# Block buffers, prepared operands and norm chains in a hybrid decoder layer

## The chip, the core and the metric

The kernel runs on one core of a Trainium2 chip. The core has a matrix engine (TensorE, PE in the profile, with its weight loads as PEld), a vector engine (VectorE, DVE), an activation engine (ScalarE, ACT), a general engine (GpSimd, POOL) and a queue engine that issues transfers (SyncE, SP). Each works through its own instructions in order and waits for others by semaphores. The metric is the device time of one execution, in microseconds (us). Three runs are given as a median with the lowest and the highest.

## The reference

One layer of a post-norm decoder over 1024 tokens of 1024 columns: a mixer of a state-space group and a gated linear attention, then a cross-attention into 256 memory tokens, then a squared-ReLU MLP of 4096 hidden columns. Each is added to the scaled residual, and the sum is normalised over its row. The end of it is what this case is about:

```
h = layer_norm(DN_ALPHA * h + memory_cross_attention(...), ln2_g, ln2_b)
ff = jnp.square(jax.nn.relu(h @ w_ff1[l])) @ w_ff2[l]
h = layer_norm(DN_ALPHA * h + ff, ln3_g, ln3_b)
```

All arithmetic is float32. A layer norm takes mean and variance of each row, multiplies the centred row by the reciprocal root of the variance (the deviation, below), then by a gain, and adds a bias.

## The kernel before

The 1024 tokens are eight tiles of 128 rows, res(0) to res(7), each 1024 columns wide. A float32 matmul is made of three: each operand is split into a high half and a low half (`split`, line 150: ScalarE copies the high half, VectorE or GpSimd subtracts it to get the low half), and `mm3` (line 160) multiplies high by high, high by low and low by high.

**The second norm** (ln2) follows the cross-attention's output product, `dense(pa, ...)` at line 1378. It runs two column halves; in each, a block of 24 matmuls for each of the eight tiles. In the second half VectorE adds each block to the residual (`post_norm`, line 1209) and calls `layer_norm` (line 224). That takes the statistics (the first half's were taken ahead), computes the deviation by eight small VectorE operations (`rsqrt1`, line 172), and normalises the tile. It shares the work: VectorE centres and scales columns, ScalarE multiplies columns 512 to 1023 by the deviation, GpSimd adds their bias. In the light form (tiles 0, 2, 4, 5, bits of GLN), ScalarE also centres them, and GpSimd multiplies by the gain.

**The up product** (line 1609) is one level of a seven-product Strassen scheme: the tokens and the hidden columns are cut in halves, and 16 groups g of hidden columns need seven products each (UP, line 1329), 12 matmuls a product. For the first eight groups (EDGE) two products, which need only the first four tiles, are made first for all (products 0 to 15), and the other five later in blocks. The last eight groups take all seven in a block. Between products 3, 6, 9 and 12 and the next ones, `x_tile` (line 1295) transposes and combines tiles 4 to 7. Each product has one weight operand, split ahead by `w1_prep` (line 1351) into a buffer of the queue `upq`. It is prepared four products ahead of its use in program order (LEADU) and its buffer is appended again after it. Three operands are prepared during the second norm (`up_first`), and seven buffers are in use: three pairs in the pool of weights, and one in the buffer named kv. Sums and differences of weights (s1, s2, s3, s4) are made by VectorE; s1 and s2 have one buffer each (w1s).

The evictions of a product follow in `up_product` (line 1410). Several products add into one bank of the accumulator after its earlier content has been read: v1 (of k = 4) and v2 (of k = 2) are such reads by VectorE, and in the first sixteen products ScalarE's copy of k = 0 is another. The squared hidden blocks go into block buffers (`hid_block`), are stored to memory, and are loaded again for the down product. Four block buffers are used to begin with, and seven from product 16 on.

**The down product** (line 1638) runs seven passes k, each of eight steps over pairs of groups. Evictions, statistics and norms are hung into these steps as a list (`pend`), one entry a step. Statistics and norms of tiles 0 to 3 (`norm_half`) go into passes 5 and 6, one tile an entry, and `behind()` puts them behind VectorE's latest instruction. Pass 6 produces tiles 4 and 5 together, then 6, then 7 in two halves of columns. `last_norm` (line 1557) normalises one tile: a chain for its deviation, then VectorE, ScalarE and GpSimd, then two stores. For tile 7 VectorE does all.

The order of each engine's instructions is not the program's order. A planner simulates the program with costs of its own, and places an instruction on its engine as soon as it takes it for ready, the one earlier in the program first. So an instruction that the planner took for ready early can stand, on the chip, ahead of one that is ready earlier.

Of the kernel before, what the change touches and what calls it, by code (L numbers as in the profile page):

```python
# [7 lines left out]
F32 = mybir.dt.float32  # L8
F32R = mybir.dt.float32r
# [8 lines left out]
P = 128  # L18
# [63 lines left out]
def hybrid_layer(  # L82
# [89 lines left out]
    def rsqrt1(y, v, eps, t):  # L172
# [4 lines left out]
        for _ in range(3):  # L177
            stt(V, w, y, vh, y, ALU.mult, ALU.mult)
            stt(V, y, w, 1.5, y, ALU.add, ALU.mult)

    ident = const.tile([P, P], F32, name="ident")
    G.memset(ident, 0.0)
    G.affine_select(out=ident, in_=ident, compare_op=ALU.not_equal, fill=1.0, base=0,
# [37 lines left out]
        rsqrt1(tq[:, 0:1], mv[:, 1:2], EPS, tq[:, 1:3])  # L221
        return mv, tq

    def layer_norm(xt, rows, light=False, st=None):
        mv, tq = norm_stats(xt, st)
        lo_, hi_ = slice(0, 512), slice(512, D)
        if light:
            stt(V, xt[:, lo_], xt[:, lo_], mv[:, 0:1], rows[:, 0, lo_], ALU.subtract, ALU.mult)
            stt(V, tq[:, 3:4], mv[:, 0:1], -1.0, tq[:, 0:1], ALU.mult, ALU.mult)
            act(xt[:, hi_], xt[:, hi_], AF.Identity, scale=tq[:, 0:1], bias=tq[:, 3:4])  # L230
            tt(G, xt[:, hi_], xt[:, hi_], rows[:, 0, hi_], ALU.mult)
        else:
            stt(V, xt, xt, mv[:, 0:1], rows[:, 0, :], ALU.subtract, ALU.mult)
            act(xt[:, hi_], xt[:, hi_], scale=tq[:, 0:1])
        stt(V, xt[:, lo_], xt[:, lo_], tq[:, 0:1], rows[:, 1, lo_], ALU.mult, ALU.add)
        tt(G, xt[:, hi_], xt[:, hi_], rows[:, 1, hi_], ALU.add)
# [757 lines left out]
    def res(t):  # L994
        return R[t // 4][:, t % 4, :]
# [213 lines left out]
    def post_norm(put, rows, scale=ALPHA, ahead=False):  # L1209

        half = stage.tile([P, NT, 2, 6], F32, tag="cn", bufs=1, name="half") if ahead else None

        def epi(n, t, po):
            r = res(t)[:, n * 512:(n + 1) * 512]
            if scale is None:
                tt(V, r, r, po, ALU.add)
            else:
                stt(V, r, r, scale, po, ALU.mult, ALU.add)
            if n == 0:
                if ahead:  # L1220
                    V.bn_stats(out=half[:, t, 0, :], in_=r)
                late.append(lambda: None)
            else:
                layer_norm(res(t), rows, GLN >> t & 1, half[:, t] if ahead else None)
                late.append(lambda: put(t))
        return epi

# [139 lines left out]
    def up_first():  # L1367

        z = wp.tile([P, 2, 2, 512], F32R, tag="w", name="w1q")
        upq.extend(z[:, i] for i in range(2))  # L1370
        upq.append(stage.tile([P, 2, 512], F32R, tag="kv", bufs=1, name="w1q"))
        w1_load(0)
        w1_load(1)
        for u in ups[:3]:
            w1_prep(*u)


# [3 lines left out]
    for _ in range(2):  # L1381
        z = wp.tile([P, 2, 2, 512], F32R, tag="w", name="w1q")
        upq += [z[:, i] for i in range(2)]
    wr_, hb_ = (wp.tile([P, 4, 512], F32, tag="w", name=n) for n in ("w1s", "hid"))
    pr1 = rowp.tile([P, 4, 512], F32, tag="row", name="pr")
    sums, v1, v2 = (wr_[:, 0], wr_[:, 1]), wr_[:, 2], wr_[:, 3]

    blocks = [hb_[:, i] for i in range(4)]
    nblk = [0]

    def hid_block():
# [162 lines left out]
            j = n * 512 // nw + i  # L1554
            V.bn_stats(out=sts[t][:, j, :], in_=res(t)[:, j * nw:(j + 1) * nw])

    def last_norm(t):
        mv = small.tile([P, 2], F32, tag="mv", name="mv")
        tq = small.tile([P, 4], F32, tag="tq2", name="tq2")
        V.bn_aggr(out=mv, in_=sts.pop(t))  # L1560
        rsqrt1(tq[:, 0:1], mv[:, 1:2], EPS, tq[:, 1:3])
        for n in range(2):
            c = slice(n * 512, (n + 1) * 512)
            r, g_, b_ = res(t)[:, c], rows3[:, 0, c], rows3[:, 1, c]
            if t == NT - 1:
                stt(V, r, r, mv[:, 0:1], g_, ALU.subtract, ALU.mult)
                stt(V, r, r, tq[:, 0:1], b_, ALU.mult, ALU.add)
            elif n == 0 or t > 3:
                stt(V, r, r, mv[:, 0:1], g_, ALU.subtract, ALU.mult)
                act(r, r, scale=tq[:, 0:1])  # L1570
                tt(G, r, r, b_, ALU.add)
            else:
                stt(V, tq[:, 3:4], mv[:, 0:1], -1.0, tq[:, 0:1], ALU.mult, ALU.mult)
                act(r, r, AF.Identity, scale=tq[:, 0:1], bias=tq[:, 3:4])
                tt(G, r, r, g_, ALU.mult)
                tt(G, r, r, b_, ALU.add)
            nc.sync.dma_start(out=out[t * P:(t + 1) * P, c], in_=r)

    def norm_half(m):
        with behind():  # L1580
            for n in range(2):
                stats(m, n)
            last_norm(m)

    nl, npr = [0], [0]

# [18 lines left out]
        edge_cells.extend(more_cells(2))  # L1605
        down_ahead(2, 2)

    nw_ = 3
    for i, (j, g, k) in enumerate(ups):
        while nw_ < len(ups) and nw_ <= i + LEADU:  # L1610
            w1_load(ups[nw_][0] + 1)
# [26 lines left out]
    for k in range(6):  # L1638
# [10 lines left out]
        for m, _, _, po in banks:  # L1649
            pend.append(lambda k=k, m=m, po=po: evict(k, m, po))  # L1650
        if k == 4:
            for m in range(2):
                pend.extend((lambda m=m: norm_half(m), lambda: None))

    def last_half(m):
        nw = 256 if m == 3 else 512
        stats(4 + m, 1, nw)

    for m in range(2):
        pend.extend((lambda m=m: norm_half(2 + m), lambda m=m: (last_half(2 * m), last_half(2 * m + 1))))  # L1660
    for ms in ((0, 1), (2,), (3,)):
        parts = [(m, c, w) for m in ms for c, w in (((0, 256), (256, 256)) if m == 3 else ((0, 512),))]
        for part in ([parts] if len(ms) == 2 else [[z] for z in parts]):
# [7 lines left out]
            for m, c, w, po in banks:  # L1671
                r = res(4 + m)[:, c:c + w]
                tt(V, r, r, po, ALU.add)
                V.bn_stats(out=sts[4 + m][:, c // w, :], in_=r)  # L1674
                if c + w == 512:
                    last_norm(4 + m)


# [31 lines left out]
```

## Time and profile before

| | |
|---|---|
| median of 3 runs | 1414.79 us (1411.76 to 1419.1) |
| the profiled execution | 1412.6 us, of which its span 1410.8 us |
| TensorE busy (matmuls) | 1341.5 us, 95% of the span |
| VectorE busy | 998.0 us, 71% |
| ScalarE busy | 570.1 us, 40% |
| GpSimd busy | 460.0 us, 33% |
| granted clock of TensorE, mean | 0.986 |

A row of the time line gives the start and the duration in us, the engine, the line of the kernel, the operation, what it writes and reads, its shape, and how often it stands there in a row. In brackets is how long the engine was idle before it, and what ended that. A helper's line (L142, L145, L148, L163) stands for all its callers, so one goes by the names of the tiles: `hl` are weights, `R` the residual, `tq` the deviation, `w1q` an operand of the up product, `w1s` the weight sums and v1 and v2, `hid` the block buffers, `pr` and `p_d` the kept first products, `xd`, `xt`, `xb` the combined tokens, `cell`, `pb` the operands of the down product. A row of the waits gives the waiting engine and what it waited for, then us in total, times, and the longest.

### The profile page before, as it was taken

To read this page: it belongs to the slowest core of one execution; us is meant where nothing else is said; L and a number is where in the kernel's file an instruction comes from. 1 tells how busy PE (TensorE), PEld (TensorE's weight loads), DVE (VectorE), ACT (ScalarE), POOL (GpSimd) and SP (SyncE) were. 2 spreads that over 40 slices of the span, in tenths; PEclk is the share of its full clock that TensorE was granted. 3 is DMA by queue.
4 is the path that set the end of the run, shared out by engine and by line. 5 is a ranking of instruction groups with operands and counts; after the bars stand their busy time and mean duration, and the time that the engine had idled before them with its cause. 6 is when DMAs were issued, how large, how long until landed. Compare 5 with 4: busy or idle time off the path is not lost. (4 is left out here: it accounts for less than half of the span.)

```text
span 1410.8 us, 18927 instructions
## 1 busy us (share of the span) xinstructions
PE 1341.5 (95%) x6824; PEld 1112.6 (79%) x6824; DVE 998.0 (71%) x1783; ACT 570.1 (40%) x946; POOL 460.0 (33%) x338
## 2 busy tenths in 40 slices
PE   7798999999899998999998999999999999999997
PEld 6575788788898887788887777778888888888886
DVE  8999588756855489844478667766555676568797
ACT  4433532342545143333123654445545343335431
POOL 1663144312855133200014223443332142003364
PEclk9899999999999999999999999999999999999999
DMA  9722342543756120310120656554446985334432
GB/s 311 255 110 81 107 121 52 161 159 112 255 186 209 56 73 23 119 30 1 60 60 23 194 174 198 194 188 142 145 140 230 343 270 178 104 105 150 149 105 90
DMA packets 155513, 199.81 MB, mean 142 GB/s; under 512 B 16294, under 2 KB 86044, under 8 KB 155292
## 3 DMA queue, kind: packets, MB, share of 16 engines
q1 hardware_dynamic: 143536, 179.44, 39.5%
q10 hardware_dynamic: 11884, 19.17, 3.7%
q8 instruction: 54, 0.88, 0.3%
q14 instruction: 39, 0.32, 0.1%
HBM read 140.38 MB, written 58.20 MB: 141 GB/s over the span
## 5 line engine op out<-in xcount | busy, mean ns | idle before, releaser
L163 PE MATMUL ps_d<-xt,w1q 128*128 128x512 f32 x576 | 138.3, 391 | 9.8 <-DVE w1s L142 9.5
L163 PEld LDWEIGHTS ps_d<-xt,w1q 128*128 128x128 f32 x576 | 107.3, 188 | 35.4 <-issue 12.2
L142 POOL TENSOR_TENSOR hl<-raw,hl 128x1024 fp32r<-128x1024 f32 x21 | 63.0, 3006 | 168.3 <-ACT hl L148 168.2
L163 PE MATMUL ps_s<-cell 128*128 128x512 f32 x432 | 113.0, 389 | 0.0
L163 PE MATMUL ps_d<-cell 128*128 128x512 f32 x432 | 106.0, 389 | 0.4 <-DVE hid L142 0.4
L142 POOL TENSOR_TENSOR R<-R,row 128x512 f32<-128x512 f32 x42 | 57.8, 1386 | 138.4 <-ACT R L148 134.9
L163 PE MATMUL ps_d<-h0T,hl 128*128 128x512 f32 x384 | 93.6, 402 | 5.8 <-DVE hl L142 5.8
L163 PE MATMUL ps_g<-xb,w1q 128*128 128x512 f32 x384 | 94.3, 397 | 3.9 <-ACT hid L148 3.9
L163 PE MATMUL ps_d<-hl,y 128*128 128x512 f32 x384 | 95.1, 403 | 2.5 <-DVE y L142 2.5
L163 PEld LDWEIGHTS ps_d<-cell 128*128 128x128 f32 x432 | 81.0, 188 | 17.6 <-DVE hid L142 0.8
L163 PEld LDWEIGHTS ps_s<-cell 128*128 128x128 f32 x432 | 81.1, 188 | 16.8
L163 PEld LDWEIGHTS ps_d<-h0T,hl 128*128 128x128 f32 x384 | 73.2, 193 | 25.8 <-DVE hl L142 6.2
L163 PE MATMUL ps_d<-hl,h0T 128*128 128x512 f32 x384 | 91.1, 393 | 1.4 <-DVE h0T L142 1.3
L148 ACT ACTIVATE hl<-raw 128x1024 fp32r<-128x1024 f32 x62 | 64.8, 1059 | 66.1 <-PE ps_d L163 60.2
L163 PE MATMUL ps_d<-hl,p 128*128 128x512 f32 x384 | 89.0, 391 | 0.0
L163 PEld LDWEIGHTS ps_g<-xb,w1q 128*128 128x128 f32 x384 | 72.5, 191 | 19.6 <-ACT hid L148 4.7
L163 PEld LDWEIGHTS ps_d<-hl,y 128*128 128x128 f32 x384 | 72.6, 193 | 18.0 <-DVE y L142 3.0
L148 ACT ACTIVATE hid<-hid 128x512 f32<-128x512 f32 x112 | 70.8, 632 | 36.9 <-DVE hid L142 35.1
L163 PEld LDWEIGHTS ps_d<-hl,h0T 128*128 128x128 f32 x384 | 71.0, 188 | 17.3 <-DVE h0T L142 1.8
L163 PEld LDWEIGHTS ps_d<-hl,p 128*128 128x128 f32 x384 | 71.6, 188 | 14.6
L142 DVE TENSOR_TENSOR cell<-ha,cell 128x1024 fp32r<-128x1024 f32 x56 | 78.2, 1401 | 5.6 <-ACT cell L148 3.4
L148 ACT ACTIVATE w1q<-raw 128x512 fp32r<-128x512 f32 x80 | 50.0, 628 | 76.2 <-PE ps_d L163 39.6
(286 smaller groups left out, 2868.8 us busy)
## 6 DMA issues: line engine op xcount, KB each, us to landing
g_d<-hid SPq DMA_DIRECT2D x112, 256.0 KB
ha<-g_d SPq DMA_DIRECT2D x56, 512.0 KB
raw<-in_w_ff_dram SPq DMA_DIRECT2D x40, 512.0 KB
b<-in_w_ff_dram SPq DMA_DIRECT2D x32, 512.0 KB
raw<-in_w_mkv_dram SPq DMA_DIRECT2D x16, 512.0 KB
raw<-in_w_in_dram SPq DMA_DIRECT2D x16, 512.0 KB
wq<-in_w_mq_dram SPq DMA_DIRECT2D x8, 512.0 KB
xs<-in_x_dram SPq DMA_DIRECT2D x8, 512.0 KB
```

The source lines that it names most:

```text
L142: e.tensor_tensor(out=o, in0=a, in1=b, op=op)
L148: A.activation(out=o, in_=i, func=f, **kw)
L163: PE.matmul(o, lhs(i), rhs(j), start=first and n == 0, stop=last and n == 2, skip_group_check=more)
```

## The change

- Up product: `up_first` prepares two operands instead of three, and kv no longer holds an operand, so that six operand buffers are in use. kv becomes two more block buffers: six to begin with, nine from product 16 on.
- Second norm: for tiles 5, 6 and 7, VectorE normalises the whole tile by two operations on 1024 columns. ScalarE and GpSimd have no part in it.
- Final norms: `last_stats` computes the deviations of several tiles in one chain (`rsqrt_n`, with nine steps of three kinds instead of six, each on as many columns as there are tiles). Tiles 0 to 3 share one, and tiles 4 and 5 share one; 6 and 7 keep a chain of their own. The statistics of tiles 0 and 1 and of 2 and 3 now stand in one entry each, and the norms of tiles 0 and 1 in the two entries after them. The second column half of tiles 0 to 3 is normalised as the first: VectorE centres and multiplies by the gain, ScalarE multiplies by the deviation, GpSimd adds the bias, where ScalarE had centred and GpSimd had multiplied by the gain.

```diff
+    def rsqrt_n(y, v, eps, t):
+        n = y.shape[1]
+        vh, w = t[:, 0:n], t[:, n:2 * n]
+        ts(V, vh, v, eps, -0.5, ALU.add, ALU.mult)
+        ts(V, y.bitcast(I32), vh.bitcast(I32), -0.5, 1597463007.0 - 2.0 ** 30 - 2.0 ** 22, ALU.mult, ALU.add)
+        for _ in range(3):
+            tt(V, w, y, y, ALU.mult)
+            tt(V, w, w, vh, ALU.mult)
+            stt(V, y, w, 1.5, y, ALU.add, ALU.mult)
...
-    def layer_norm(xt, rows, light=False, st=None):
+    def layer_norm(xt, rows, light=False, st=None, alone=False):
         mv, tq = norm_stats(xt, st)
         lo_, hi_ = slice(0, 512), slice(512, D)
+        if alone:
+            stt(V, xt, xt, mv[:, 0:1], rows[:, 0, :], ALU.subtract, ALU.mult)
+            stt(V, xt, xt, tq[:, 0:1], rows[:, 1, :], ALU.mult, ALU.add)
+            return
...
-                layer_norm(res(t), rows, GLN >> t & 1, half[:, t] if ahead else None)
+                layer_norm(res(t), rows, GLN >> t & 1, half[:, t] if ahead else None, ahead and t > 4)
...
-        upq.append(stage.tile([P, 2, 512], F32R, tag="kv", bufs=1, name="w1q"))
         w1_load(0)
         w1_load(1)
-        for u in ups[:3]:
+        for u in ups[:2]:
             w1_prep(*u)
...
+    hk_ = stage.tile([P, 2, 512], F32, tag="kv", bufs=1, name="hid")
...
-    blocks = [hb_[:, i] for i in range(4)]
+    blocks = [hb_[:, i] for i in range(4)] + [hk_[:, i] for i in range(2)]
...
-    def last_norm(t):
-        mv = small.tile([P, 2], F32, tag="mv", name="mv")
-        tq = small.tile([P, 4], F32, tag="tq2", name="tq2")
-        V.bn_aggr(out=mv, in_=sts.pop(t))
-        rsqrt1(tq[:, 0:1], mv[:, 1:2], EPS, tq[:, 1:3])
+    def last_stats(ts_):
+        n = len(ts_)
+        mv = small.tile([P, 16], F32, tag="dg", bufs=2, name="mvn")[:, 0:8].rearrange("p (t c) -> p t c", c=2)
+        tq = small.tile([P, 12], F32, tag="sq", name="tqn")
+        for i, t in enumerate(ts_):
+            V.bn_aggr(out=mv[:, i], in_=sts.pop(t))
+        if n == 1:
+            rsqrt1(tq[:, 0:1], mv[:, 0, 1:2], EPS, tq[:, 4:6])
+        else:
+            rsqrt_n(tq[:, 0:n], mv[:, 0:n, 1], EPS, tq[:, 4:4 + 2 * n])
+        return [(t, mv[:, i, 0:1], tq[:, i:i + 1]) for i, t in enumerate(ts_)]
+
+    def last_norm(t, mean, rstd):
         for n in range(2):
             c = slice(n * 512, (n + 1) * 512)
             r, g_, b_ = res(t)[:, c], rows3[:, 0, c], rows3[:, 1, c]
+            stt(V, r, r, mean, g_, ALU.subtract, ALU.mult)
             if t == NT - 1:
-                stt(V, r, r, mv[:, 0:1], g_, ALU.subtract, ALU.mult)
-                stt(V, r, r, tq[:, 0:1], b_, ALU.mult, ALU.add)
-            elif n == 0 or t > 3:
-                stt(V, r, r, mv[:, 0:1], g_, ALU.subtract, ALU.mult)
-                act(r, r, scale=tq[:, 0:1])
-                tt(G, r, r, b_, ALU.add)
+                stt(V, r, r, rstd, b_, ALU.mult, ALU.add)
             else:
-                stt(V, tq[:, 3:4], mv[:, 0:1], -1.0, tq[:, 0:1], ALU.mult, ALU.mult)
-                act(r, r, AF.Identity, scale=tq[:, 0:1], bias=tq[:, 3:4])
-                tt(G, r, r, g_, ALU.mult)
+                act(r, r, scale=rstd)
                 tt(G, r, r, b_, ALU.add)
             nc.sync.dma_start(out=out[t * P:(t + 1) * P, c], in_=r)
...
-    nw_ = 3
+    nw_ = 2
...
         if k == 4:
-            for m in range(2):
-                pend.extend((lambda m=m: norm_half(m), lambda: None))
+            pend.extend(lambda m=m: (half_stats(m), half_stats(m + 1)) for m in (0, 2))
+            pend.extend(norm_half for _ in range(2))
...
-        pend.extend((lambda m=m: norm_half(2 + m), lambda m=m: (last_half(2 * m), last_half(2 * m + 1))))
+        pend.extend((norm_half, lambda m=m: (last_half(2 * m), last_half(2 * m + 1))))
...
-                if c + w == 512:
-                    last_norm(4 + m)
+            if banks[-1][1] + banks[-1][2] == 512:
+                for z in last_stats([4 + m for m in ms]):
+                    last_norm(*z)
```

`half_stats(m)` takes the statistics of tile m, and with tile 3 the joint chain; `norm_half()` normalises the next of the four tiles.

More of the change, by code (lines that the diff above doesn't have):

```diff
@@ L1564, in last_norm, with half_stats @@
             r, g_, b_ = res(t)[:, c], rows3[:, 0, c], rows3[:, 1, c]
+            stt(V, r, r, mean, g_, ALU.subtract, ALU.mult)
             if t == NT - 1:
-                stt(V, r, r, mv[:, 0:1], g_, ALU.subtract, ALU.mult)
-                stt(V, r, r, tq[:, 0:1], b_, ALU.mult, ALU.add)
-            elif n == 0 or t > 3:
-                stt(V, r, r, mv[:, 0:1], g_, ALU.subtract, ALU.mult)
-                act(r, r, scale=tq[:, 0:1])
-                tt(G, r, r, b_, ALU.add)
-            else:
-                stt(V, tq[:, 3:4], mv[:, 0:1], -1.0, tq[:, 0:1], ALU.mult, ALU.mult)
-                act(r, r, AF.Identity, scale=tq[:, 0:1], bias=tq[:, 3:4])
-                tt(G, r, r, g_, ALU.mult)
+                stt(V, r, r, rstd, b_, ALU.mult, ALU.add)
+            else:
+                act(r, r, scale=rstd)
                 tt(G, r, r, b_, ALU.add)
             nc.sync.dma_start(out=out[t * P:(t + 1) * P, c], in_=r)
-    def norm_half(m):
+    first = []
+    def half_stats(m):
         with behind():
@@ L1582, in norm_half @@
                 stats(m, n)
-            last_norm(m)
+            if m == 3:
+                first.extend(last_stats(range(4)))
+    def norm_half():
+        with behind():
+            last_norm(*first.pop(0))
     nl, npr = [0], [0]
```

## The prediction

> **What bounds the kernel now.** First the page: TensorE's matmuls are busy 95% of the span. So only a stretch in which TensorE stands still, or runs at a lower clock, has anything to give. Then the stretches of the stages that the change touches: the start of the up product, its blocks of five products, its blocks of seven (columns: us, PE, PEld, DVE, ACT and POOL busy with counts, granted clock, DMA share, GB/s).
>
> ```profile
> span 1410.8 us, 18927 instructions
> ...
> PE 1341.5 (95%) x6824; PEld 1112.6 (79%) x6824; DVE 998.0 (71%) x1783; ACT 570.1 (40%) x946; POOL 460.0 (33%) x338
> ```
>
> ```profile
> 772.30:775.96 3.66, 0.00 (x0) 0.00 (x0) 3.45 (x9) 1.77 (x4) 1.72 (x2) 1.00 0.01 3
> 775.96:777.50 1.54, 1.54 (x4) 1.25 (x5) 1.54 (x2) 1.51 (x3) 0.60 (x1) 0.51 0.68 196
> 840.00:930.00 90.00, 80.45 (x350) 64.90 (x349) 67.26 (x82) 39.28 (x63) 33.74 (x23) 1.00 0.62 196
> 930.00:1083.00 153.00, 152.79 (x671) 125.46 (x671) 87.61 (x119) 77.10 (x127) 58.69 (x42) 1.00 0.47 155
> ```
>
> TensorE is idle for 3.66 us at the start and then gets half its clock (0.51); it loses 9.55 us in the blocks of five and 0.2 us in those of seven. Third, TensorE's own waits from 760 to 1411 us name what it waited for:
>
> ```profile
> PE ps_g L163 <- ACT hid L148: 3.9, 2, 3.7
> PE ps_s L1303 <- ACT xd L148: 1.7, 1, 1.7
> PE ps_d L163 <- DVE w1s L142: 9.5, 6, 1.6
> PE ps_d L163 <- DVE hid L142: 0.4, 1, 0.4
> ```
>
> These four, 15.5 us, are all of TensorE's waits there. None names a store of a hidden block. The time line shows the first:
>
> ```profile
> 763.44 5.60 PE L163 MATMUL ps_g<-xb,w1q 128*128 128x512 f32 x24
> ...
> 767.48 0.72 ACT L148 ACTIVATE R<-R,tq 128x512 f32<-128x512 f32 x1 [5.75 <-DVE tq L145]
> 768.63 0.58 ACT L148 ACTIVATE hid<-ps_g 128x512 f32<-128x512 f32 x1
> 774.18 0.72 ACT L148 ACTIVATE R<-R,tq 128x512 f32<-128x512 f32 x1 [3.93 <-DVE tq L145]
> 775.33 0.58 ACT L148 ACTIVATE hid<-ps_g 128x512 f32<-128x512 f32 x1
> 775.96 4.61 PE L163 MATMUL ps_g<-xb,w1q 128*128 128x512 f32 x12 [3.66 <-ACT hid L148]
> 780.41 0.60 PE L1303 MATMUL ps_s<-ident,xd 128*128 128x128 f32 x4
> ...
> 783.46 0.66 PE L1303 MATMUL ps_s<-ident,R 128*128 128x128 f32 x4
> ```
>
> ScalarE stands at its half of the second norm's tiles 6 and 7, waiting for VectorE's deviation (tq). Behind that instruction is queued the eviction (hid<-ps_g) of a bank that TensorE has to add to. From 775.96 to 780.41 twelve matmuls take 4.45 us where a product takes 2.72 (989.08 to 991.80, quoted below): 1.73 us more, from the half clock. The gap costs 0.22 + 3.66 + 1.73 = 5.6 us, where 0.22 is the rest of the row's 3.9.
>
> **Second norm, tiles 5 to 7 by VectorE alone.** The bypass takes from ScalarE three halves, and from GpSimd four additions or products (tile 5 has two). VectorE gets whole-tile second operations. The rows for their cost:
>
> ```profile
> 742.03 1.28 DVE L145 SCALAR_TENSOR_TENSOR R<-R,mv,row 128x1024 f32<-128x1024 f32 x1
> 760.77 2.68 POOL L142 TENSOR_TENSOR R<-R,row 128x512 f32<-128x512 f32 x2 [6.15 <-ACT R L148]
> 762.17 2.35 DVE L145 SCALAR_TENSOR_TENSOR R<-R,mv,row 128x1024 f32<-128x1024 f32 x1
> 775.46 2.25 DVE L142 TENSOR_TENSOR w1q<-raw,w1q 128x512 fp32r<-128x512 f32 x2
> ```
>
> Alone on the ports a whole tile costs 1.28 us; a half costs 0.70 (1.41 for two, the 1406.24 row below). Tile 5 pays 2 x 1.28 for 2 x 0.70 and a small step (0.22, a sixth of the 1.30 below): +0.9. Tiles 6 and 7 pay 1.28 for 0.70: +0.6 each, so +2.1 for VectorE. Against it, 2.35 is what the same 1024 columns took while GpSimd worked on its half of tile 5 (760.77), 1.07 more than alone; and the two at 775.46 took 2.25 while GpSimd added its half of tile 7, 0.87 more than twice 0.69 (the 855.08 row). GpSimd now makes operands earlier, so I count half of the first and all of the second: net +0.7. The ends are +0.2 (both come back) and +6.4 (neither does, and each of the four added whole-tile operations meets GpSimd and takes 2.35).
>
> Before, VectorE's backlog ends at 777.7 (775.46 + 2.25); now at 778.4. The two evictions that TensorE waits for no longer stand behind a norm: their banks are full at 766.2 and 768.9, one and two products after 763.44. TensorE then runs two more products, to 774.3, and meets tile 4's transposes. The fourth of them came 3.05 us after the first (780.41 to 783.46), which would be 777.4; it needs a bank that VectorE reads, behind the backlog, at 778.5. What is late next is this bank, by 1.1 us, with ends of 0.5 and 6.8. Saved: 5.6 - 1.1 = **4.5 us**, between 5.1 and -1.2. ScalarE and GpSimd only lose work.
>
> [...]
>
> **Two prepared operands.** The third operand's high half on ScalarE and its low half on GpSimd now come where the fourth's stood:
>
> ```profile
> 760.59 1.14 ACT L148 ACTIVATE w1q<-raw 128x512 fp32r<-128x512 f32 x2
> 763.40 2.27 POOL L142 TENSOR_TENSOR w1q<-raw,w1q 128x512 fp32r<-128x512 f32 x1
> 765.70 0.37 SPq L1347 DMA_DIRECT2D raw<-in_w_ff_dram  x1
> ```
>
> Two of them, even at 2.27 each after 761.3, are done at 765.9. TensorE needs the third at 768.9 and the fourth at 771.6. Cover: two products; without it, 2.27 us. The first weight buffer is held until then, so the fifth load leaves at the time of the 765.70 row rather than near 720, and is first needed by the ninth product, past 785. Cost here 0.
>
> In the steady blocks the pool of operands is six instead of seven, and each preparation waits for a bank of operands that is released one product later. One five-product block:
>
> ```profile
> 851.72 0.63 ACT L148 ACTIVATE w1q<-w1s 128x512 fp32r<-128x512 f32 x1 [0.47 <-PE ps_d L163]
> 853.29 1.75 POOL L142 TENSOR_TENSOR w1q<-w1s,w1q 128x512 fp32r<-128x512 f32 x1
> 854.46 2.88 PE L163 MATMUL ps_s<-xt,w1q 128*128 128x512 f32 x12
> 855.08 0.69 DVE L142 TENSOR_TENSOR w1s<-raw 128x512 f32<-128x512 f32 x1 [0.59 <-POOL w1q L142]
> 856.41 1.77 DVE L142 TENSOR_TENSOR raw<-raw 128x512 f32<-128x512 f32 x1
> 858.11 0.68 DVE L142 TENSOR_TENSOR w1s<-ps_d,pr 128x512 f32<-128x512 f32 x1
> 858.93 2.97 PE L163 MATMUL ps_d<-xt,w1q 128*128 128x512 f32 x12 [1.58 <-DVE w1s L142]
> ```
>
> VectorE's order puts two weight sums and a difference (855.08 to 858.1) ahead of the eviction v1 (858.11), whose bank was full at 854.4; they waited for GpSimd to have read the old sum (853.29). TensorE loses 1.58 us, six times: 9.5. With six operands 851.72 becomes about 854.5. Its low half ends between 856.4 (1.29 on GpSimd, nothing ahead) and 858.1 (ScalarE's squares of 1.3 us first). The sums follow v1 then, and TensorE's third product starts at 857.2 without a wait. Late next is the eviction v2 of the product at 854.46, wanted at 859.9: behind both sums and the difference (0.69 + 0.69 + 0.68 to 1.77) it ends between 859.1 and 862.0, ahead of the difference up to 1 us earlier. So the wait that takes the other's place is 0 to 2.1 us. I take 0.9, the nearer to the lower end, as the planner can put v2 before the difference. Saved: 6 x (1.58 - 0.9) = **4.1 us**, between -3 and +9.5.
>
> **Six block buffers.** Seven then nine blocks where there were four then seven. As no wait names a store, they bring 0; a longer queue of free blocks can add no wait either. The last bank of the down product takes the block buffer's place a whole pass after its last store: 0.
>
> **Final norms.** One chain for tiles 0 to 3 and one for 4 and 5, where each had its own. Half of tiles 0 to 3 moves from a biased ScalarE operation and two GpSimd ones to VectorE (0.70 each), ScalarE and one GpSimd one.
>
> ```profile
> 1357.82 44.31 PE L163 MATMUL ps_d<-pb,cell 128*128 128x512 f32 x240
> 1402.17 0.42 DVE L142 TENSOR_TENSOR R<-R,ps_d 128x256 f32<-128x256 f32 x1 [4.39 <-PE ps_d L163]
> 1404.90 1.30 DVE L145 SCALAR_TENSOR_TENSOR tq<-tq 128x1 f32<-128x1 f32 x6
> 1406.24 1.41 DVE L145 SCALAR_TENSOR_TENSOR R<-R,tq,row 128x512 f32<-128x512 f32 x2
> ```
>
> On VectorE six chains of six steps go (6 x 1.30), two of nine come (2 x 9 x 0.22, with 0.22 a sixth of 1.30), and 4 x 0.70 is paid: 1.0 us less. All of it, and the stores on SP's queue, lies beside matmuls without a gap (1357.82); tile 7, alone at the end, keeps its instructions from 1402.17 on. VectorE is idle 4.39 us before that. Cost 0; without that cover, up to 3 us of VectorE.
>
> **The sum.** The profiled execution took 1412.6 us for a span of 1410.8, 2.2 below the median 1414.8 of the runs. 4.5 + 4.1 = 8.6 less: 1404.0 against its own time, **1406** against the median.
>
> **The rivals.** (1) The start is won, but the blocks' wait only moves from v1 to v2: -4.5, 1410. For it: both have one product of slack. (2) VectorE is the bound at the start: with two of the four added whole tiles at 2.35 and nothing back (2.1 + 2 x 1.07) the backlog ends at 781.9, TensorE meets it at tile 4's bank 4.6 us late instead of 1.1, and the blocks stay: 5.6 - 4.6 = 1.0, 1414. Against it: GpSimd has four operations less. [...] (3) All waits go, x_tile's 1.7 too: 5.1 + 9.5 + 1.7, 1399. (4) Slower, in the blocks of seven:
>
> ```profile
> 989.08 2.88 PE L163 MATMUL ps_g<-xb,w1q 128*128 128x512 f32 x12
> 989.37 0.69 DVE L142 TENSOR_TENSOR w1s<-raw 128x512 f32<-128x512 f32 x1 [2.05 <-DMA raw<-in_w_ff_dram]
> 990.71 0.68 DVE L142 TENSOR_TENSOR w1s<-ps_d,pr 128x512 f32<-128x512 f32 x1
> 991.80 2.88 PE L163 MATMUL ps_d<-xt,w1q 128*128 128x512 f32 x12
> ```
>
> Here VectorE waits 2.05 us for a weight load, and v1, behind the sum, ends 0.4 us before the product that needs it. The load waits for its buffer, which a preparation now frees a product (2.72) later. If the sum stays ahead of v1, each of eight blocks loses 2.3 us: 18.4 - 4.5 = +13.9, 1429. It decides where the order is kept; against it, the sum must itself wait for the later low half of the old one, and so should fall behind v1.
>
> **How the numbers follow.** Forecast 0.44 (its own range 1401 to 1410), (1) 0.20, (2) 0.12, (3) 0.10, (4) 0.14. A change below 0.5%, 7 us, can't be told from none. Faster: 0.10 + 0.32 of the forecast + 0.05 of (1) = 0.47. Slower: (4) and 0.02 of (2), where the backlog costs more than it gives: 0.16. Same: 0.37. From 1397 to 1418 only (4) and 0.04 of (3) lie outside.
>
> **What would show it.** The row of TensorE waiting for ACT hid falls from 3.9 to under 1, and the clock stays 1.00 near 776. The wait for w1s (9.5) falls to about 5 and is one on ps_s, or stays on ps_d if the order is kept. The blocks of seven lose under 1 us in 153; over 10 is rival (4). The last matmul to the end stays at 8.7 us. A wait for a store of hid, or a gap in the down product, would prove me wrong.

## The result, and the profile after

The changed kernel takes **1400.25 us** (median of 6 runs, 1396.52 to 1403.48) beside 1415.59 us for the kernel before on the same chip: a ratio of 0.989, 95% interval 0.987 to 0.991. That is 15 us faster, where 8.6 were forecast. The profiled execution took 1396.5 us, the fastest of the six. The page's head and its busy times:

```profile
span 1394.7 us, 18871 instructions
...
PE 1336.5 (96%) x6824; PEld 1108.8 (80%) x6824; DVE 976.8 (70%) x1756; ACT 567.2 (41%) x943; POOL 447.2 (32%) x330
```

The span is 16.1 us shorter. Where it went is read by cutting both traces at the same three places: the first product of the up product, the first product after the sixteen early ones, and the first product of the blocks of seven; the last cut is the end of the last matmul. Columns as in the prediction. Before:

```profile
763.44:822.63 59.19, 53.64 (x257) 43.41 (x256) 44.67 (x74) 36.79 (x68) 17.49 (x12) 0.97 0.51 161
822.63:942.66 120.03, 110.48 (x482) 89.56 (x480) 85.68 (x108) 54.76 (x89) 46.49 (x31) 1.00 0.58 186
942.66:1402.13 459.47, 458.84 (x2065) 380.62 (x2063) 314.32 (x363) 200.04 (x254) 149.22 (x89) 1.00 0.50 169
```

After:

```profile
762.23:816.15 53.92, 51.68 (x257) 42.36 (x256) 44.78 (x73) 34.36 (x64) 11.88 (x9) 1.00 0.58 179
816.15:926.79 110.64, 110.41 (x481) 89.62 (x480) 72.88 (x109) 54.22 (x89) 44.27 (x30) 1.00 0.64 206
926.79:1386.11 459.32, 458.38 (x2065) 380.68 (x2063) 306.20 (x337) 199.81 (x255) 145.94 (x86) 1.00 0.50 169
```

The first sixteen products take 5.3 us less (59.19 to 53.92), the blocks of five **9.4 us** less (120.03 to 110.64), all that follows 0.15 less. The up product begins 1.2 us earlier, before almost all of the changed code; equal code differs by more than that between executions, as the traces below show, so nothing is read into it. Together 16.0. The middle row carries the lesson: TensorE's 480 matmuls are as busy as before (110.4), and VectorE, with the same operations (108 and 109), is busy **12.8 us less** (85.68 to 72.88). Its instructions became shorter, not fewer.

TensorE's waits from 740 us on, after:

```profile
PE ps_s L1318 <- ACT xd L148: 2.2, 4, 0.7
PE ps_d L163 <- DVE hid L142: 0.9, 2, 0.5
```

The 3.9 us for ScalarE's eviction and the 9.5 us for VectorE's are gone. What there is of the bank that was to be late next stands in the time line of the start:

```profile
762.23 11.05 PE L163 MATMUL ps_g<-xb,w1q 128*128 128x512 f32 x48
765.52 0.58 ACT L148 ACTIVATE hid<-ps_g 128x512 f32<-128x512 f32 x1
...
774.11 1.28 DVE L142 TENSOR_TENSOR w1q<-raw,w1q 128x512 fp32r<-128x512 f32 x2
776.68 0.66 PE L1318 MATMUL ps_s<-ident,R 128*128 128x128 f32 x4 [0.47 <-ACT xd L148]
```

Four products run without a gap (48 matmuls in 11.05 us, at a granted clock of 1.00), the two evictions (765.52 and 768.24) follow their products at once, and the transposes of tile 4 meet a bank that is 0.47 us late. VectorE's backlog ends at 775.4, 13.2 us after the first product; before it was 14.3 (777.7 less 763.44).

One block of five products after, in which v1 is `w1s<-ps_d,pr` and v2 is `w1s<-ps_s,pr`:

```profile
846.50 0.69 DVE L142 TENSOR_TENSOR w1s<-ps_d,pr 128x512 f32<-128x512 f32 x1 [0.27 <-PE ps_d L163]
847.86 1.29 POOL L142 TENSOR_TENSOR w1q<-w1s,w1q 128x512 fp32r<-128x512 f32 x1
849.02 2.88 PE L163 MATMUL ps_d<-xt,w1q 128*128 128x512 f32 x12
849.18 0.69 DVE L142 TENSOR_TENSOR w1s<-raw 128x512 f32<-128x512 f32 x1 [1.99 <-POOL w1q L142]
850.51 0.69 DVE L142 TENSOR_TENSOR raw<-raw 128x512 f32<-128x512 f32 x1
851.12 0.68 DVE L142 TENSOR_TENSOR w1s<-ps_s,pr 128x512 f32<-128x512 f32 x1
851.95 3.01 PE L163 MATMUL ps_s<-xb,w1q 128*128 128x512 f32 x12
852.42 1.75 POOL L142 TENSOR_TENSOR w1q<-raw,w1q 128x512 fp32r<-128x512 f32 x1 [3.28 <-ACT w1q L148]
```

v1 now stands ahead of the sums, so the product at 849.02 doesn't wait. The sums and the difference follow, at 0.69 us each: GpSimd stands idle for 3.28 us, from 849.15 to 852.42, just while VectorE runs them. Before, the same difference took 1.77 us beside a GpSimd subtraction of hidden blocks. v2 ends at 851.80, and the product that reads its bank starts at 851.95, 0.2 later than 849.02 plus 2.72.

### The profile page after: what moved, and what is told of

It reads as the page before. It is cut to its first block, busy times and chain, and to the rows that moved or that the text cites. A ratio compares the mean times of both kernels' runs of the same rounds, so it can differ in the third digit from the quotient of the medians.

```text
span 1394.7 us, 18871 instructions
## 1 busy us (share of the span) xinstructions
PE 1336.5 (96%) x6824; PEld 1108.8 (80%) x6824; DVE 976.8 (70%) x1756; ACT 567.2 (41%) x943; POOL 447.2 (32%) x330
## 5 line engine op out<-in xcount | busy, mean ns | idle before, releaser
L142 POOL TENSOR_TENSOR R<-R,row 128x512 f32<-128x512 f32 x34 | 45.9, 1361 | 143.1 <-ACT R L148 140.0
L142 DVE TENSOR_TENSOR cell<-ha,cell 128x1024 fp32r<-128x1024 f32 x56 | 84.5, 1511 | 3.2 <-ACT cell L148 3.2
```

The source lines that it names most:

```text
L142: e.tensor_tensor(out=o, in0=a, in1=b, op=op)
```

## The experiments

The table gives each kernel's ratio to the kernel before on its chip, and the three stages of its profiled execution as cut above (us). The last column is their sum less that of before, 638.7.

| kernel | ratio (95%) | first 16 | blocks of five | rest | sum, less before |
|---|---|---|---|---|---|
| before | 1 | 59.2 | 120.0 | 459.5 | 0 |
| after | 0.989 (0.987 to 0.991) | 53.9 | 110.6 | 459.3 | -14.8 |
| e1_no_alone | 0.995 (0.993 to 0.998) | 59.7 | 115.5 | 459.0 | -4.5 |
| e2_seven_ops | 0.998 (0.995 to 1.000) | 56.6 | 120.2 | 459.3 | -2.7 |
| e3_four_blocks | 0.988 (0.984 to 0.993) | 53.7 | 111.0 | 459.1 | -15.0 |
| e4_old_final | 0.988 (0.984 to 0.992) | 53.9 | 111.0 | 459.3 | -14.5 |
| e6_t5 | 0.990 (0.988 to 0.993) | 57.8 | 110.7 | 459.1 | -11.1 |
| e7_t3 | 0.988 (0.985 to 0.990) | 53.1 | 110.8 | 459.7 | -15.0 |
| e8_five_ops | 0.993 (0.990 to 0.996) | 53.5 | 115.7 | 458.0 | -11.5 |
| e5_sums_behind | 0.997 (0.994 to 0.999) | 58.5 | 119.8 | 458.8 | -1.6 |
| e9_order | 0.998 (0.997 to 1.000) | 59.2 | 118.7 | 458.6 | -2.2 |
| e10_gp | 0.999 (0.997 to 1.001) | 60.3 | 120.2 | 458.6 | +0.5 |
| e11_order_t3 | 0.994 (0.992 to 0.996) | 58.2 | 118.7 | 459.7 | -2.1 |
| e12_no_gp | 0.991 (0.989 to 0.994) | 59.2 | 108.8 | 459.5 | -11.2 |

In before, e5, e9 and e12 the work ahead of the up product is the same, yet it begins at 763.4, 768.1, 764.5 and 768.5 us. So differences of some 5 us between two profiled executions mean nothing there, and the stages are compared instead. Each stage is one execution's; where the code is the same (the blocks of five in after, e3 and e4), they agree within 0.4 us.

**The parts, each undone.** First the norm of tiles 5 to 7, shared between the engines again (e1):

```diff
-                layer_norm(res(t), rows, GLN >> t & 1, half[:, t] if ahead else None, ahead and t > 4)
+                layer_norm(res(t), rows, GLN >> t & 1, half[:, t] if ahead else None)
```

> The changed kernel with the second norm's tiles 5 to 7 shared by three engines again, as before. Theory: the start's gap alone comes back (TensorE waits for ACT hid 3 to 4 us, then runs at half clock for some 3 us), the blocks of five stay without a wait: 5 to 6 us over the changed kernel, 1405 to 1406. Rival (the norm's new place in the plan also moved the order of the blocks): the wait for w1s comes back too, 15 us over, near 1415.

Then the operands: the third prepared one and the one in kv come back, and kv's two block buffers go (e2):

```diff
+        upq.append(stage.tile([P, 2, 512], F32R, tag="kv", bufs=1, name="w1q"))
-        for u in ups[:2]:
+        for u in ups[:3]:
...
-    blocks = [hb_[:, i] for i in range(4)] + [hk_[:, i] for i in range(2)]
+    blocks = [hb_[:, i] for i in range(4)]
...
-    nw_ = 2
+    nw_ = 3
```

> The changed kernel with the buffer kv as an operand again: three prepared, seven operand buffers, four and then seven block buffers, as before. Theory: the start stays won, the wait for w1s of 9.5 us comes back: 1409 to 1410. Rival (the norm's move or the final norms removed the blocks' wait): no wait for w1s, within 2 us of 1400.

Measured: e1 1409.31 us, e2 1412.82 us. TensorE's waits from 740 us on, e1 and then e2:

```profile
PE ps_g L163 <- ACT hid L148: 4.4, 2, 2.8
PE ps_s L163 <- DVE w1s L142: 3.2, 6, 0.6
```

```profile
PE ps_d L163 <- DVE w1s L142: 9.6, 6, 1.6
PE ps_s L1318 <- ACT xd L148: 3.4, 2, 2.7
```

The norm takes away the gap at the start, and six operands take away the wait for v1: each part undone brings its own wait back. But the parts don't add. e1, which keeps the operands, saves 4.5 us in the blocks of five (120.0 to 115.5); e2, which keeps the norm, saves nothing there (120.2); both together save 9.4. In e1 TensorE waits for v2 in six blocks, 0.5 us each.

Now the block buffers alone (e3: the list of e2 with kv unused) and the final norms alone (e4: `last_stats`, `last_norm` and the entries of the list as before):

```diff
-    blocks = [hb_[:, i] for i in range(4)] + [hk_[:, i] for i in range(2)]
+    blocks = [hb_[:, i] for i in range(4)]
```

> The changed kernel with four and then seven block buffers, and the buffer kv unused; six operand buffers as in the changed one. Theory (block buffers bring nothing): no wait for w1s, within 2 us of 1400. Rival (the two more block buffers removed the blocks' wait): the wait of 9.5 us comes back, 1409 to 1410.

```diff
-            if banks[-1][1] + banks[-1][2] == 512:
-                for z in last_stats([4 + m for m in ms]):
-                    last_norm(*z)
+                if c + w == 512:
+                    last_norm(4 + m)
```

> The changed kernel with the final norms of before: a chain for each tile, GpSimd with two operations in the second half of tiles 0 to 3. Theory (all of it lies beside matmuls): no wait of TensorE in the down product, the same 8.6 us from the last matmul to the end, within 2 us of 1400. Rival (the joint chains gave a part of the gain): 2 to 5 us over the changed kernel, with a gap in the last 80 us.

1400.25 and 1400.04 us: without either, the kernel is as fast as with it. Both parts bring nothing that can be measured.

**How many tiles, how many operands.** VectorE alone for tiles 6 and 7 only (e6), for 4 to 7 (e7), and five operands, prepared three products ahead (e8):

```diff
-                layer_norm(res(t), rows, GLN >> t & 1, half[:, t] if ahead else None, ahead and t > 4)
+                layer_norm(res(t), rows, GLN >> t & 1, half[:, t] if ahead else None, ahead and t > 5)
```

> The changed kernel with only tiles 6 and 7 of the second norm done by VectorE alone; tile 5 shared as before. Theory (ScalarE stood before the evictions at tiles 6 and 7 only): no wait for ACT hid, within 2 us of 1400. Rival (tile 5's GpSimd work delays VectorE by contention, and VectorE the transposed tiles): TensorE's wait for xd grows from 2.2 to over 4 us, 1402 to 1405.

e7 is the same line with `t > 3`.

> The changed kernel with tile 4, too, normalised by VectorE alone. Theory (VectorE's backlog is what TensorE meets next, at tile 4's transposes): 0.7 us more of VectorE, the wait for xd grows by up to 1 us, within 2 us of 1400. Rival (VectorE waited 2 us for GpSimd's half of tile 4 near 754, so this frees it): the wait for xd of 2.2 us falls below 1, 1398 to 1400.

```diff
-LEADU = 4
+LEADU = 3
...
+    upq.pop()
     nw_ = 2
```

> The changed kernel with five operand buffers, prepared three products ahead instead of four. Theory (an operand fewer shifts the preparation by another product, to a place in the block that the plan adapts to, with two products of lead left): VectorE's v1 stays ahead of the sums, a few us of new waits for operands or weight loads at most, 1399 to 1405. Rival (the weight loads, released a product later, stand before an eviction): a wait of 1 to 2.5 us in each block of five or seven, 1410 to 1435.

e6 measured 1402.59 us. Its blocks keep their gain (110.7), its first sixteen products lose 3.9 us of theirs, and the wait for the transposes' bank is 4.4 us instead of 2.2. The rest of the 3.9 is TensorE's pace: behind a wait of 2.99 us, 29 matmuls take 8.46 us instead of 6.87 (the 29 at 777.09 after). (The runs alone don't show the loss: the ratio, 0.990, isn't clear of the change's 0.989.) VectorE has less to do than after (tile 5 is shared again), yet its backlog ends 15.7 us after the first product (782.42 less 766.73) instead of 13.2. VectorE in e6 while GpSimd adds its half of tile 5 and makes three low halves from 764.05 to 771.97:

```profile
765.46 2.34 DVE L145 SCALAR_TENSOR_TENSOR R<-R,mv,row 128x1024 f32<-128x1024 f32 x1
...
767.90 2.32 DVE L145 SCALAR_TENSOR_TENSOR tq<-tq 128x1 f32<-128x1 f32 x2
```

A whole tile takes 2.34 us instead of 1.28, and two steps on a single column take 2.32, where six took 1.30. So here, taking GpSimd out of tile 5 gives VectorE more than the tile costs it.

e7 measured 1398.86 us, the lowest median of all, but its ratio 0.9876 (0.9853 to 0.9898) can't be told from the 0.9887 of the change itself. e8 measured 1406.97 us: the blocks lose 5.0 of their 9.4 us to evictions into hidden blocks:

```profile
PE ps_d L163 <- DVE hid L142: 4.9, 7, 1.1
```

So fewer operands is not better by itself: beside six, seven lose 9.6 us here (e2), and five with the shorter lead lose 5.

**Is it the order of VectorE's instructions?** From the kernel before, with seven operands, the sums were put behind v1 in two ways. e5 hangs them behind VectorE's latest instruction of the program, e9 just behind the v1 of two blocks earlier (`v1_at` keeps that instruction for each group):

```diff
+            with behind():
-            tt(V, r["s1"], r["a21"], r["a22"], ALU.add)
-            tt(V, r["s2"], r["s1"], r["a11"], ALU.subtract)
+                tt(V, r["s1"], r["a21"], r["a22"], ALU.add)
+                tt(V, r["s2"], r["s1"], r["a11"], ALU.subtract)
```

> The kernel before, with one thing changed: the two weight sums s1 and s2 are put on VectorE behind the VectorE instruction that precedes them in the program, which in a block of five is the eviction v1. Seven operands, four blocks, old norms. Theory (the order of the sums and v1 on VectorE made the 9.5 us): TensorE's wait for w1s on ps_d goes, the start's 3.9 us stay: 9 us under the kernel before, 1405 to 1407. Rival (the number of operands itself matters, and the sums are only late with it): a wait of like size stays, on ps_d or ps_s, within 3 us of 1415.

```diff
+            with tc.issue_after(v1_at[g - 2]) if 2 <= g < EDGE + 2 else nullcontext():
-            tt(V, r["s1"], r["a21"], r["a22"], ALU.add)
-            tt(V, r["s2"], r["s1"], r["a11"], ALU.subtract)
+                tt(V, r["s1"], r["a21"], r["a22"], ALU.add)
+                tt(V, r["s2"], r["s1"], r["a11"], ALU.subtract)
```

> The kernel before, with one order changed: in the blocks of five, the weight sums s1 and s2 that stood just ahead of an eviction v1 on VectorE are put just behind the same v1. Seven operands, four and then seven block buffers, old norms. Theory (that place alone made the 9.5 us, whatever the number of operands): the wait for w1s on ps_d goes and at most 3 us come as a wait on ps_s; the start's gap stays: 7 to 9 us under the kernel before. Rival (with seven operands the sums are then too late, as they were when put a whole block later): 6 us or more of waits for an operand, within 3 us of the kernel before.

e5 measured 1413.19 us and e9 1413.26 us. In e5 the sums came so late that the operand itself was missed (7.8 us of TensorE waiting for ScalarE's high half); it says little. e9 is the cleaner test. Its longest wait:

```profile
PE ps_s L163 <- DVE w1s L142: 8.0, 7, 1.3
```

The wait on ps_d for v1 is gone and has become one on ps_s for v2, nearly as long. VectorE in one block of e9, with the GpSimd operation at 857.98:

```profile
854.73 0.69 DVE L142 TENSOR_TENSOR w1s<-ps_d,pr 128x512 f32<-128x512 f32 x1 [0.17 <-PE ps_d L163]
856.45 1.37 DVE L142 TENSOR_TENSOR w1q<-raw,w1q 128x512 fp32r<-128x512 f32 x1 [1.03 <-ACT w1q L148]
857.98 1.59 POOL L142 TENSOR_TENSOR w1q<-raw,w1q 128x512 fp32r<-128x512 f32 x1 [0.71 <-ACT w1q L148]
858.45 1.67 DVE L142 TENSOR_TENSOR w1s<-w1s,raw 128x512 f32<-128x512 f32 x1
860.64 0.68 DVE L142 TENSOR_TENSOR w1s<-ps_s,pr 128x512 f32<-128x512 f32 x1
```

v1 stands first (854.73), as after. But operations that take 0.69 us after take 1.37 and 1.67 here, and v2 comes late. The rest of the order isn't that of after either: the planner put a low half (856.45, behind 1.03 us of waiting for ScalarE) ahead of the sums. By an estimate from these rows, at 0.69 us each the same operations in this order would end v2 at 859.7, ahead of 859.97, when TensorE could use it (857.25, where the product before begins, plus 2.72). So putting the sums behind v1 is not enough; the durations are the other half.

**Is it GpSimd?** e12 is the kernel before with its own order, without two GpSimd subtractions of hidden blocks in each block of five (it leaves out a part of the layer's arithmetic):

```diff
-            tt(G, x_, h["a11"], x_, ALU.subtract)
+            if g >= EDGE:
+                tt(G, x_, h["a11"], x_, ALU.subtract)
...
-            tt(G, h["s4"], h["a12"], h["s2"], ALU.subtract)
+            if g >= EDGE:
+                tt(G, h["s4"], h["a12"], h["s2"], ALU.subtract)
+            else:
+                h["s4"] = h["a12"]
```

> The kernel before without GpSimd's two subtractions of hidden blocks (s3 and s4) in the blocks of five: s3 is stored unsubtracted and s4 as a copy of a12, so that the output is not the layer's. VectorE's order is the same. Theory (VectorE is late because it meets GpSimd on the memory's ports: 11.66 us busy in a block of the kernel before, 9.46 in one of the changed kernel, for the same operations): the pair hid<-hid falls from 2.61 to 1.42 us, raw<-raw from 1.77 to 0.69, and the wait for w1s from 9.5 us to under 3: 6 to 9.5 us under the kernel before. Rival (the sums wait for GpSimd's low half, and that order alone is the cause): the durations stay, and with them half of the wait or more, within 5 us of the kernel before.

1406.52 us, a ratio of 0.991 (0.989 to 0.994), and the wait for w1s is gone whole. Its blocks of five, and two rows of VectorE in one of them:

```profile
827.69:936.51 108.82, 108.82 (x482) 90.09 (x480) 69.13 (x108) 54.77 (x89) 22.93 (x17) 1.00 0.64 206
```

```profile
858.37 0.68 DVE L142 TENSOR_TENSOR raw<-raw 128x512 f32<-128x512 f32 x1
858.97 0.68 DVE L142 TENSOR_TENSOR w1s<-ps_d,pr 128x512 f32<-128x512 f32 x1
```

TensorE has no idle time at all there. VectorE has the same 108 operations as before and in the old order, v1 behind both sums and the difference, and is busy 69.13 us instead of 85.68. The old order would have been good enough. Two things came together before, each from GpSimd. The difference took 1.77 us beside a subtraction and takes 0.68 alone: 1.1 us. And GpSimd's low half, behind a subtraction on its queue and longer beside VectorE (1.75 us where it takes 1.29 at 847.86 after), ended 0.58 us after the start of the product at 854.46 (853.29 and 1.75); here it ends 0.62 before the like product: 1.2 us, by which the sums start earlier. By these sums neither alone covers the wait of 1.58 us; together they do.

The pairs `hid<-hid`, two VectorE operations on hidden blocks, show the same. VectorE's groups from 845 to 925 us, before, after, and e12:

```profile
L142 DVE TENSOR_TENSOR hid<-hid 128x512 f32<-128x512 f32 x10 | 12.6, 1258 | 4.3 <-ACT hid L148 3.8
L142 DVE TENSOR_TENSOR raw<-raw 128x512 f32<-128x512 f32 x5 | 8.9, 1772 | 0.0
```

```profile
L142 DVE TENSOR_TENSOR hid<-hid 128x512 f32<-128x512 f32 x10 | 6.9, 692 | 4.0 <-ACT hid L148 3.8
L142 DVE TENSOR_TENSOR raw<-raw 128x512 f32<-128x512 f32 x6 | 4.1, 686 | 0.0
```

```profile
L142 DVE TENSOR_TENSOR hid<-hid 128x512 f32<-128x512 f32 x12 | 8.3, 693 | 4.8 <-ACT hid L148 4.6
```

1258 ns before, 692 after with every GpSimd subtraction still there, 693 with them left out. GpSimd does as much work after (44.3 us in the blocks of five, 46.5 before), but not so as to hold up VectorE. The second operation of the pair and GpSimd's first subtraction are both released by the first of the pair. Before:

```profile
852.05 1.29 POOL L142 TENSOR_TENSOR hid<-hid 128x512 f32<-128x512 f32 x1 [8.20 <-DVE hid L142]
852.06 1.82 DVE L142 TENSOR_TENSOR hid<-hid 128x512 f32<-128x512 f32 x1
...
855.90 1.74 POOL L142 TENSOR_TENSOR hid<-hid 128x512 f32<-128x512 f32 x1 [0.85 <-ACT hid L148]
857.91 1.40 POOL L142 TENSOR_TENSOR w1q<-raw,w1q 128x512 fp32r<-128x512 f32 x1 [0.28 <-ACT w1q L148]
```

After:

```profile
857.77 0.69 DVE L142 TENSOR_TENSOR hid<-hid 128x512 f32<-128x512 f32 x1
857.82 1.80 POOL L142 TENSOR_TENSOR hid<-hid 128x512 f32<-128x512 f32 x1 [3.65 <-DVE hid L142]
```

In these two meetings the engine that begins first takes its usual time, and the other takes longer: VectorE before (1.82 instead of 0.69), GpSimd after (1.80 instead of 1.29). GpSimd's second subtraction, at 855.90 before, lies over the difference at 856.41; after, it comes ahead of the low half and is done before VectorE's sums. That the first meeting is decided by hundredths of a microsecond (852.05 to 852.06, 857.77 to 857.82) is what the rows show. It falls the same way in every block of after and in six of the eight of before; the first and the last pair there (835.77 and 942.19) took 1.42 us, as after. What tips it was not found.

**Is the gap at the start ScalarE's queue?** From the kernel before, GpSimd multiplies the high half of tiles 6 and 7 by the deviation in ScalarE's stead (e10):

```diff
-            act(xt[:, hi_], xt[:, hi_], scale=tq[:, 0:1])
+            if st is not None and gp_mult:
+                ts(G, xt[:, hi_], xt[:, hi_], tq[:, 0:1])
+            else:
+                act(xt[:, hi_], xt[:, hi_], scale=tq[:, 0:1])
```

> The kernel before, with one thing moved: in tiles 6 and 7 of the second norm GpSimd, and not ScalarE, multiplies columns 512 to 1023 by the deviation. VectorE has as much to do as before. Theory (TensorE's gap at the start came from ScalarE standing at the norm ahead of the evictions): the wait for ACT hid goes, the clock stays 1.00, and 2 to 5 us come off, as VectorE's backlog is still met at tile 4's transposes. Rival (VectorE's backlog itself is the bound, ScalarE only shows it): the 5.6 us come back as a wait for xd, within 1 us of the kernel before.

1413.9 us, no change that can be measured. Beside the 9.6 us for v1, TensorE now waits here:

```profile
PE ps_s L1306 <- ACT xd L148: 6.1, 2, 3.8
```

The wait for ScalarE's eviction is gone, so ScalarE standing at the norm was the cause of the gap. But the stage got no shorter (60.3 us). VectorE's backlog, longer beside a busier GpSimd (it ends at 785.68, 15.0 us after the first product), stops tile 4's transposes for 2.26 us. Then tile 5's are stopped for 3.82 us by something else: VectorE stands 4.57 us at a weight sum whose weights are still being loaded, and the read that frees their bank stands behind it. The four transposes behind it take 1.12 us instead of the 0.66 at 786.96, and the 28 matmuls after them 9.01, where 29 take 6.87 at 814.21. So taking away the gap gains only where neither the backlog nor this sum takes its place.

**The norm and the order without the operands.** Last, e9's order together with VectorE alone for tiles 4 to 7, on the kernel before (e11):

```diff
-                layer_norm(res(t), rows, GLN >> t & 1, half[:, t] if ahead else None)
+                layer_norm(res(t), rows, GLN >> t & 1, half[:, t] if ahead else None, ahead and t > 3)
```

> The kernel before with the order of e9 (sums behind v1) and with the second norm's tiles 4 to 7 by VectorE alone; seven operands, three prepared, four and then seven block buffers, old final norms. Theory (place of the sums and ScalarE's queue are the whole gain, and neither the number of operands, nor the block buffers, nor the final norms count): no wait for ACT hid, under 3 us of waits in the blocks of five, 1398 to 1402. Rival (six operands bring something of their own): 3 us or more over the changed kernel's 1400.

1407.81 us, ratio 0.994 (0.992 to 0.996): faster than before, slower than after. Its blocks of five are those of e9 (118.7), so six operands bring what neither this order nor this norm brought. Part of e11 stays open: its runs gained 8.7 us, its stages show 2.1. Elsewhere the two agree within 3 us. Its profiled execution, at 1416.1 us, was the slowest of its ten, and no row tells where the others were faster. In it TensorE waits 4.18 us at tile 5's transposes, where VectorE stands 5.57 us at the weight sum named under e10; whether that is as long in the other nine is not known.

## Why the prediction was right or wrong

- **Second norm: right, its price for VectorE wrong in sign.** The gap and the half clock went (granted 1.00 over the first sixteen products, 0.97 before), and what was late next was the bank for tile 4's transposes: 0.47 us instead of 1.1. The first sixteen products gained 5.3 us where 4.5 were forecast. The forecast counts the 1.73 us of the half clock as wholly saved beside a rest of 1.1 us; that the clock stays whole behind such a rest was the author's estimate, and no run shows it at this place. The runs showed 1.00 from 776.68 to 781.00, behind the 0.47 us of after, and 1.00 from 840 to 930 us of before, with waits of up to 1.6 us. The term that was mis-sized is VectorE's net cost, +0.7, which put the end of its backlog 15.0 us after the first product. Measured were 13.2, 1.1 less than before. The forecast counted half of one stretched row as coming back, and only the rows that were stretched before; the small steps of a deviation's chain were stretched too (2.32 us for two of them in e6, where six take 1.30). Tile 5, which looked dearest (+0.9), is worth 3.9 us in e6's trace.
- **Two prepared operands at the start: put at 0, which missed a wait.** e2, with three, takes 2.6 us more in the first sixteen products than after. The rows of e2:

```profile
795.76 0.69 DVE L142 TENSOR_TENSOR w1s<-raw 128x512 f32<-128x512 f32 x1 [4.12 <-DMA raw<-in_w_ff_dram]
...
798.95 1.00 PE L1318 MATMUL ps_s<-ident,R 128*128 128x128 f32 x4 [2.72 <-ACT xd L148]
```

  VectorE's order puts a weight sum ahead of its reads of tile 5's transposes. The sum waits for its weights, TensorE waits 2.72 us for the bank, and then is slow: the four transposes take 1.00 us and the 28 matmuls behind them 8.01, where a tile later four take 0.66 and 29 take 6.86. The same sum waits 3.07 us before (that is x_tile's 1.7), 4.57 in e10 and 5.57 in e11, all with three prepared and seven buffers. After, it stands behind these reads (791.43, they begin at 785.73), and the wait there is 0.35. So the prediction saw the sums' place in the blocks and overlooked it at the start. As e2 changes the whole plan of that stage, it isn't shown that the third operand alone makes that order.
- **Six operands in the blocks of five: the step right, its reason only half.** v1 was freed, the sums followed it, and v2 was late next, as the prediction put it. The mis-sized term is the wait that takes the other's place: 0.9 us was taken from 0 to 2.1, about 0.2 was measured, and the 5 us that should have stayed of the wait for w1s are no longer in the list. So a block fell from 15.4 us to 13.9 and the stage gained 9.4 us instead of 4.1. The reason given for 0.9, that the planner can put v2 ahead of the difference, did not come true: v2 (851.12) stands behind it (850.51). The 2.1 had in it a difference of 1.77 us, as if that were its length; it was its length beside a GpSimd subtraction, which after comes earlier. e9 shows that v1 ahead of the sums without this ends as rival (1) had it, with 8.0 us of waits for v2.
- **The sum.** The forecast had 4.5 and 4.1; measured are 5.3 and 9.4. The time, 1400.25, lies just outside the forecast's own 1401 to 1410, next to rival (3)'s 1399. It is rival (3) but for x_tile's waits: the one of 1.7 us went, and four short ones, 2.2 together, came. That rival had a chance of only 0.10. It was priced low because the range's lower end was held for a lucky case, when it was what the operations cost alone.
- **That the two gains are independent: wrong.** The sum added them. Undone one at a time, the operands without the norm gain 4.5 us in the blocks, and the norm without the operands gains none there. Nor does the norm alone keep its whole gain at the start (2.6 us in e2, 5.3 in after). The norm's work ends before the blocks, and in the blocks of e1 at 849 us and of after at 846 us VectorE, ScalarE and GpSimd have the same order. What differs is one meeting. In e1:

```profile
852.91 1.60 POOL L142 TENSOR_TENSOR w1q<-raw,w1q 128x512 fp32r<-128x512 f32 x1 [2.81 <-ACT w1q L148]
853.27 1.78 DVE L142 TENSOR_TENSOR raw<-raw,w1s 128x512 f32<-128x512 f32 x1
```

  After, VectorE begins this difference at 852.32, ahead of GpSimd's 852.42, and takes 0.68 us. In e1 it comes 0.36 us behind GpSimd, takes 1.78, and what hangs on it is late: the pair on hidden blocks begins 2.6 us ahead of the next product on ps_s (858.73 to 861.35), after 3.2 us ahead (857.05 to 860.23). So v2 is late again, and so is the next difference. What sets this going in e1 was not tried; in its first block of five the sums waited for a weight load until 835.55, 5.8 us after the block's first product, where after it was 5.1.
- **Block buffers and final norms: 0, right** (e3, e4). The last matmul to the end takes 8.6 us, before 8.7.
- **The blocks of seven: right.** They lose 0.94 us in 153 (forecast under 1). Rival (4) fell by the argument given: v1 has moved ahead of the sum, which can't begin before GpSimd's low half (done at 994.04) and here waits on for its weight load.

```profile
992.27 0.69 DVE L142 TENSOR_TENSOR w1s<-ps_d,pr 128x512 f32<-128x512 f32 x1 [1.36 <-PE ps_d L163]
...
995.24 0.69 DVE L142 TENSOR_TENSOR w1s<-raw 128x512 f32<-128x512 f32 x1 [2.28 <-DMA raw<-in_w_ff_dram]
```

- **Rival (2)**, VectorE as the bound at the start, did not come with this change. It came where GpSimd kept or got work in the norm: a wait of 2.99 us in e6, and 2.26 of the 6.1 in e10.

## What to carry to other kernels

Before a row's duration goes into a sum, look at what GpSimd does in those microseconds: here an operation that took 1.77 us, where its like took 0.69, lay beside one of GpSimd, and an edit that shifted one of the two engines ended that. So a wait for VectorE can be cured by taking work from GpSimd or by moving it, and giving VectorE a whole tile can end its backlog sooner. When one wait is taken away, look in the same stage for an operation that waits for a load ahead of an eviction. When two edits meet in one planned schedule, time each without the other before adding their gains.

## What the runs showed of the hardware

**How long VectorE takes beside GpSimd.** In these rows an operation of VectorE that reads two tiles and begins while GpSimd works ends a fixed time after GpSimd does: the difference of before at 858.18, GpSimd at 857.64 (855.90 and 1.74), 0.54 us later; in e9 the sum at 860.12, GpSimd at 859.57 (857.98 and 1.59), 0.55 later. From 700 to 1090 us of before and after, 55 single rows of `TENSOR_TENSOR` on VectorE, 128x512 and reading no bank, begin while a row of GpSimd runs: 52 of them end 0.54 to 0.56 us behind it and take 0.71 to 1.82 us, where one alone takes 0.69. So how long such a row is depends on when GpSimd's ends, not on its own size: two steps on one column took 2.32 us in e6 instead of 0.43 (a third of 1.30). An eviction, which reads a bank and one tile, shows nothing of this: v1 at 858.11 before took 0.68 us, all of it within GpSimd's operation from 857.91 to 859.31, and 53 single rows of that size and stretch that read a bank beside GpSimd take 0.68 or 0.69. Which of the two is longer when both begin within hundredths does not follow from the starts alone: at 852.06 VectorE begins 0.01 us behind GpSimd and takes 1.82, at 798.98 before it begins 0.03 behind and takes 0.68, and GpSimd 1.87. The prediction priced such rows as slower work and asked how much would come back; the question to ask was which of VectorE's rows would begin beside one of GpSimd. No run shows the ports that it and the expectation of e12 name; the runs show the times.

**The half clock after a gap of 2.2 us.** The same product of an earlier stage, with the same matmuls in front and almost the same gap ahead of it, in the kernel before and then after:

```profile
325.10 4.63 PE L163 MATMUL ps_d<-mnT,hl 128*128 128x256 f32 x24 [2.22 <-DVE wqT L142]
326.60:328.10 1.50, 1.50 (x9) 1.50 (x9) 1.46 (x3) 0.00 (x0) 0.00 (x0) 0.50 0.83 315
```

```profile
325.47 3.13 PE L163 MATMUL ps_d<-mnT,hl 128*128 128x256 f32 x24 [2.21 <-DVE wqT L142]
325.47:327.00 1.53, 1.53 (x13) 1.53 (x13) 1.53 (x2) 0.00 (x0) 0.00 (x0) 1.00 0.95 296
```

Before, the product got a clock of 0.50, after one of 1.00. In e10 the matmuls behind a gap of 2.26 us kept their pace too (29 in 6.84 us, and 6.87 at 814.21 without a gap); in e1 one of 2.70 (780.40 to 783.10) was followed by 0.51 and 0.50 for 3.2 us, where behind a gap of 1.57 one product earlier it had stayed at 1.00. So of these three gaps of 2.2 us one brought the half clock and two did not: such a gap must be reckoned with. The ones of 1.6 us named here did not bring it.
